# Layer 0's adaLN weights by column groups, and five tiles' latents summed with features outermost

## The chip, the cores and the metric

The kernel runs on one core of a Trainium2 chip, as one launch. A core has a matrix engine (TensorE, PE in the profile, with weight loads listed apart as PEld), three engines for elementwise work (VectorE or DVE, ScalarE or ACT, GpSimd or POOL), and SyncE (SP), whose queue issues most of the transfers between the chip's memory and the core's on-chip memory. The metric is the device time of the launch in microseconds; lower is better.

## The reference, cut to what matters

A two-layer diffusion backbone over 1024 latent tokens and 256 context tokens, 1024 features wide. Each layer modulates its input with a shift and a scale that come out of a conditioning vector; the context has a vector of its own.

```python
def adaln(cvec, w, b):
    m = jax.nn.silu(cvec) @ w + b                    # w: 1024 x 3072, b: 3072
    return jnp.split(m, 3, axis=-1)                  # shift, scale, gate

shift, scale, gate = adaln(c, ada_w[i], ada_b[i])
shift_c, scale_c, gate_c = adaln(c_ctx, ada_w[i], ada_b[i])
h = x * (1.0 + scale[:, None, :]) + shift[:, None, :]
h_c = ctx * (1.0 + scale_c) + shift_c
...
# layer 0, multi-head latent attention
q_lat, kv_lat, k_pe, gate = jnp.split(t @ w_in, splits, axis=-1)     # 256, 128, 32, 1024 columns
q = (rms_norm(q_lat, g_qa) @ w_qb).reshape(bsz, n, A_HEADS, A_NOPE + A_ROPE)
kv = (rms_norm(kv_lat, g_kva) @ w_kvb).reshape(bsz, n, A_HEADS, A_NOPE + A_V)
```

For this document the first steps of layer 0 matter: the shift and the scale of both vectors, h for all 1280 tokens, and the first 416 columns of `h @ w_in`, called the latents. The gates (the other 1024 columns), the attention, and layer 1 (differential attention) follow and are the same in both kernels.

## The kernel before

All matrix work of layer 0 up to here is in f32 accuracy: each operand is split into a high part, rounded for TensorE's fast f32 mode, and a low part, the rest. One product is three matmuls (`mm3`, lines 216 to 219: high x high, high x low, low x high).

The 1280 tokens are 10 tiles of 128: tiles 0 to 7 the latents of the image, 8 and 9 the context. Features are 8 blocks of 128, k = 0 to 7. h is held transposed, features on the partitions: `hH` and `hL`. Its parts come in three chunks of tokens (`CHUNKS`): 0 to 511 (tiles 0 to 3), 512 to 1023 (tiles 4 to 7) and the 256 context tokens. One part (`h_part`, line 286) is a load, ScalarE's modulation into `hH` (line 292), the same sum once more by VectorE (293), and a subtraction into `hL` (295) on VectorE, or GpSimd for every third k.

The order before:

- The adaLN weights come by rows: for each k a tile of 128 x 1024 for the scale, then one for the shift (line 254, `adaw`, a ring of 6). One row block holds all columns, so no scale and no shift is complete before the last block is there. The scale is summed by TensorE (line 260), 8 matmuls of 128 x 128 each block, as a column over the partitions; the bias enters by matmuls over one row (line 243). The shift is summed by VectorE (line 264), two products of 1024 columns for each k, one for each vector, into `hacc`; line 273 turns it into columns with 8 matmuls for each vector. `cols0` holds the finished columns.
- The input weights (`in_weight`, line 245, 128 x 416 each) come between, split into `wAH` (line 208) and `wAL` (line 209).
- Then h of the context, the first half of tile 8's latents (`lat_mm`, line 279: for a tile, for each k, one `mm3`), the image's shift, h of the first chunk, and the second half.
- A loop over the tiles 8, 9, 0, ..., 7 then sums a tile's 24 latent matmuls, normalises it (lines 405 to 412: squares on ScalarE, a power on GpSimd, products on VectorE) and, three tiles later, turns it (`lat_post`, transposes in lines 378 and 379 into a bank of kind c, of which there are two; copy in 380, subtraction in 381, copy in 384, and a small store in 385). In the same loop the second chunk of h is made and the first gate weights are loaded (`gate_w`, line 353). The last three turns alternate with the first three gate tiles (`gate_tile`, 24 matmuls of 256 columns).
- Then come the remaining gate tiles, each beside one step of side work: the up weights (line 428 on, their column sums in line 450) and layer 1's adaLN (`ada_dve`).

Order: in this part TensorE's instructions stay in the order of the program (`manual_schedule`, `MAN = 'P'`). Those of the other engines and of SP's queue are placed by the framework's scheduler, by priority (program order, raised inside `high_priority`) and its own estimate of when operands are ready. On the chip each of them runs in that fixed order. A tile from a ring (`bufs`) is written again once its readers are done.

## Time and profile before

| What | Value |
|---|---|
| Median of three runs | 1677.8 us (1677.79 to 1680.78) |
| Profiled execution, its own time | 1678.12 us |
| Its span in the profile | 1676.3 us |
| TensorE busy | 1610.6 us, 96% of the span |
| VectorE, ScalarE, GpSimd busy | 1264.0, 1144.2, 908.8 us |
| Mean granted clock of TensorE | 0.993 |
| Transfers over the span | 171.63 MB, mean 102 GB/s |
| adaLN weight loads of layer 0 | 16 of 512 KB |

How to read it: times in the views are microseconds from the start of the span. L260 is line 260 of the kernel before. A row such as `PE ps_c L260 <- DMA adaw<-in_ada_w: 4.8, 3, 2.7` says that TensorE's instruction of that line waited for that transfer, 4.8 us in all, three times, at most 2.7 us. A row of a group ends with its busy time, the mean of one in ns, the idle time of the engine before it and what ended it. A row of stretches gives the stretch, its length, the busy time and the count of instructions for each engine, the granted clock, the busy share of the 16 DMA engines, and GB/s. A matmul in f32 shows as two records. Neighbouring records of TensorE overlap, since each includes the time until its result is out.

### The profile page before, as it was taken

The numbers are of one execution on the slowest core, as the hardware profiler recorded it, in microseconds if no ns is written. First come the engines' busy times: TensorE is split into PE (matmuls) and PEld (weight loads), VectorE is DVE, ScalarE is ACT, GpSimd is POOL, SyncE is SP. The second block draws the span as 40 slices with busy tenths as digits, with TensorE's granted clock in tenths as the row PEclk, the third lists the DMA queues.
The fourth block names the chain that finished last, engine by engine and source line by source line (L and its number), as shares of the span: only waits on it lengthen the run. The fifth ranks groups of instructions, "written<-read, shape, count | busy, mean of one in ns | idle before, by whom it ended". The sixth has DMA issues, their size and how long they took to land.

```text
span 1676.3 us, 36592 instructions
## 1 busy us (share of the span) xinstructions
PE 1610.6 (96%) x14308; PEld 1205.2 (72%) x14308; DVE 1264.0 (75%) x2005; ACT 1144.2 (68%) x2228; POOL 908.8 (54%) x772
## 2 busy tenths in 40 slices
PE   7999999999999999989999999999999999996998
PEld 6999966666666666667776686767686868674776
DVE  7657856776676766855763989999889889888685
ACT  2652148878888788936554888878788787877352
POOL 1523027877777777855644526262635454555565
PEclk9999999999999999999999999999999999998999
DMA  9347620111111121346533244444443333253542
GB/s 319 91 132 232 206 81 21 42 33 42 39 36 42 39 52 45 104 167 204 177 113 79 72 101 102 102 102 105 98 95 86 96 84 92 59 156 89 146 135 76
DMA packets 183932, 171.63 MB, mean 102 GB/s; under 512 B 82024, under 2 KB 159432, under 8 KB 183759
## 3 DMA queue, kind: packets, MB, share of 16 engines
q1 hardware_dynamic: 175886, 161.96, 35.1%
q10 hardware_dynamic: 7872, 7.34, 1.3%
q8 instruction: 112, 1.84, 0.5%
q14 instruction: 62, 0.50, 0.1%
HBM read 98.65 MB, written 27.07 MB: 75 GB/s over the span
## 4 chain that ended last, share of the span: by engine, by line
PE 65%; DVE 19%; ACT 9%; issue 3%; DMA 2%; POOL 2%; POOLq 0%; DVEq 0%; SPq 0%; ACTq 0%
PE ps_s L217 5%; PE ps_s L219 5%; PE ps_s L218 5%; PE ps_a L969 4%; PE ps_a L970 4%; PE ps_a L971 4%; PE ps_a L217 3%; PE ps_a L219 3%; PE ps_a L218 3%; ACT p L1874 3%; PE ps_a L920 3%; DVE mx L1867 3%; DVE p L1887 3%; PE ps_d L994 2%; PE ps_d L987 2%
## 5 line engine op out<-in xcount | busy, mean ns | idle before, releaser
L979 POOL TENSOR_TENSOR pl<-p,ph 128x1024 f16<-128x1024 f32 (+1 forms) x176 | 370.2, 2117 | 102.7 <-ACT ph L977 68.6
L975 ACT ACTIVATE p<-ps_a,esc 128x1024 f32<-128x1024 f32 (+1 forms) x176 | 188.7, 1072 | 58.9 <-PE ps_a L971 52.4
L924 DVE TENSOR_REDUCE mx<-ps_a 128x1 f32<-128x1024 f32 x128 | 156.2, 1222 | 72.1 <-PE ps_a L920 71.5
L1874 ACT ACTIVATE p<-ps_p,mx 128x512 f32<-128x512 f32 x256 | 175.5, 689 | 31.4 <-DVE mx L1869 30.6
L977 ACT CAST ph<-p 128x1024 f16<-128x1024 f32 (+1 forms) x176 | 177.0, 1006 | 7.0 <-PE ps_d L988 1.8
L1867 DVE TENSOR_REDUCE mx<-ps_p 128x1 f32<-128x512 f32 x256 | 164.2, 680 | 1.9 <-PE ps_p L1846 1.9
L969 PE MATMUL ps_a<-qH,KH 100*128 100x512 f16 x320 | 122.0, 381 | 3.1 <-DVE mx L924 2.3
L970 PE MATMUL ps_a<-qH,KL 96*128 96x512 f16 x320 | 121.5, 380 | 0.0
L971 PE MATMUL ps_a<-qL,KH 96*128 96x512 f16 x320 | 120.7, 377 | 0.0
L1795 DVE SCALAR_TENSOR_TENSOR pl<-ps_t,lcf,ph 128x512 f16<-128x512 f32 (+1 forms) x128 | 78.2, 611 | 42.5 <-ACT ph L1793 41.9
L1887 DVE SCALAR_TENSOR_TENSOR p<-p,sm,p 128x1280 f32<-128x1280 f32 x64 | 106.1, 1658 | 1.7
L1845 PE MATMUL ps_p<-KS,QS 128*128 128x512 f16 x256 | 98.1, 383 | 9.5 <-ACT p L1874 9.5
L987 PE MATMUL ps_d<-Vh,ph 128*128 128x65 f16 x1344 | 103.7, 194 | 2.0 <-ACT ph L977 1.7
L988 PE MATMUL ps_d<-Vl,ph 128*128 128x64 f16 x1344 | 103.2, 194 | 0.0
L1793 ACT ACTIVATE ph<-ps_t,lcf 128x512 f16<-128x512 f32 (+1 forms) x128 | 74.8, 584 | 39.3 <-PE ps_t L1788 38.1
L1846 PE MATMUL ps_p<-KS,Q 128*128 128x512 f16 x256 | 98.2, 383 | 0.0
L987 PEld LDWEIGHTS <-ph 128*128 128x128 f16 x1344 | 89.0, 98 | 11.2 <-issue 4.8
L988 PEld LDWEIGHTS <-ph 128*128 128x128 f16 x1344 | 87.3, 98 | 3.8
L191 POOL TENSOR_SCALAR ss<-ss 128x1 f32<-128x1 f32 x64 | 20.4, 318 | 119.1 <-ACT ps_t L1817 117.4
L920 PE MATMUL ps_a<-KH,qH 96*128 96x512 f16 x256 | 76.1, 379 | 0.0
L936 DVE TENSOR_REDUCE mx<-ps_a 128x4 f32<-128x1024 f32 (+1 forms) x48 | 50.3, 1048 | 33.9 <-PE ps_a L931 33.9
L1810 PE MATMUL ps_t<-vh,ph 128*128 128x128 f16 x384 | 68.4, 221 | 6.4 <-DVE pl L1795 6.3
(503 smaller groups left out, 5573.3 us busy)
## 6 DMA issues: line engine op xcount, KB each, us to landing
ws<-in_dw SPq DMA_DIRECT2D x28, 512.0 KB, 3.9
adw<-in_ada_w SPq DMA_DIRECT2D x24, 512.0 KB, 4.5
adaw<-in_ada_w SPq DMA_DIRECT2D x16, 512.0 KB, 6.8
g<-sg_d SPq DMA_DIRECT2D x16, 512.0 KB, 3.5
sg_d<-gg ACTq DMA_DIRECT2D x40, 128.0 KB, 2.9
o_d<-op SPq DMA_DIRECT2D x7, 640.0 KB, 3.8
xt<-in_xT SPq DMA_DIRECT2D x16, 256.0 KB, 3.7
wgs<-in_w_in SPq DMA_DIRECT2D x32, 128.0 KB, 2.9
```

Source lines behind the costliest of these rows:

```text
L924: add("m.max", "D", 1.223, lambda t=t, ps=ps: dve.tensor_reduce(mx.tile[:, t, 0:1], ps.tile, axis=AX.X, op=ALU.max), r=[ps], w=[(mx, t)] i ...
L969: pe.matmul(s_, KH[i][:nr, ks], QH.tile[:nr, :], start=True, stop=False)
L970: pe.matmul(s_, KL[i][:DQ, ks], QH.tile[:DQ, :], start=False, stop=False)
L971: pe.matmul(s_, KH[i][:DQ, ks], QLo.tile[:DQ, :], start=False, stop=True)
L975: add("s.exp", "A", 1.114 if x else 0.682, lambda st=st, p32=p32: act.activation(p32.tile[:, :2 * n], st.tile[:, :2 * n], AF.Exp, scale=esc0),
L977: add("s.hi", "A", 1.046 if x else 0.618, lambda p32=p32, ph=ph: act.copy(ph.tile[:, :2 * n], p32.tile[:, :2 * n]), r=[p32], new=[ph], hol ...
L979: add("s.lo", "G", 2.14 if x else 1.17, lambda p32=p32, ph=ph, pl=pl: pool.tensor_tensor(pl.tile[:, :2 * n], p32.tile[:, :2 * n], ph.tile[ ...
L987: pe.matmul(v_()[:, t, :], w, Vh[:, k, h, :], start=(k == kcs[0] and t == 0), stop=False, skip_group_check=True)
L988: pe.matmul(v_()[:, t, :V0], w, Vl[:, k, h, :], start=False, stop=False, skip_group_check=True)
L1867: add(f"max{m}", "D", 0.68, lambda i=i, b_=b_: dve.tensor_reduce(mx.tile[:, 2 + 2 * m + i:3 + 2 * m + i], b_.tile, axis=AX.X, op=ALU.max, ...
L1874: add(f"exp{m}", "A", 0.78 if n == 512 else 0.57, lambda i=i, c0=c0, n=n, b=b, lo=lo: act.activation(p[m].tile[:, c0:c0 + n], b.tile[:, lo ...
L1887: add("join", "D", 1.65, lambda: dve.scalar_tensor_tensor(p[0].tile, p[1].tile, sm.tile[:, 4:5], p[0].tile, op0=ALU.mult, op1=ALU.add), r= ...
```

## The change

The features form five groups, given as first block and number of blocks: (0, 1), (1, 1), (2, 2), (4, 2), (6, 2). For a group only the columns of its features are loaded, over all 1024 rows (`ada_load`): tiles of 128 x 1024 as before, but a row of a transfer is 128 or 256 numbers, 512 or 1024 bytes, instead of 4 KB. The ring has 7 tiles.

- A group's scale is summed on TensorE, 8 matmuls for each block. For the first three groups (features 0 to 3) the shift is too. For the last two, VectorE sums the shift with high priority, 16 products of 256 columns for each group, and TensorE turns it with matmuls of one column.
- The bias comes as 16 rows of 128, is turned once, and is added when the sums leave PSUM. The matmuls of line 243, the four warm-up matmuls of line 301 and `shift_cols` go.
- Behind each group follow, for each of its features, the input weight, h of the context and h of the first chunk. For odd features GpSimd makes `wAL` and subtracts for `hL`; ScalarE makes the second modulation of the first chunk. The second chunk of h follows for all features.
- Five tiles (8, 9, 0, 1, 2) have a bank of their own from the start, and a feature's latent matmuls are issued for all five once the next group's adaLN sums have been issued; a group of two adds its own first feature's. Features 6 and 7 come last.
- Tiles 3 to 7 are summed after that, one by one, as before. Between them come turns of earlier tiles; four turns stand in a row after tile 7, then one gate tile, then the last two turns. Each turn takes two steps of the gate weights instead of one.
- The side work begins at the fourth gate tile, as before, by a test on the count of gate tiles.

The diff:

```diff
@@ -228,60 +228,79 @@
 
     hs_ctx = ExitStack()
     hs = hs_ctx.enter_context(spool("hstage", side="right"))
-    rowb = hs.tile([P, D], F32, tag="adaw", bufs=6, name="rowb")[0:1, :]
-    acc = [hs.tile([P, D], F32, name=f"hacc{s}") for s in range(2)]
-    sp.dma_start(rowb, ada_b[0:1, D:2 * D])
-    for s in range(2):
-        pool.memset(acc[s], 0.0)
+    GROUPS = (0, 1), (1, 1), (2, 2), (4, 2), (6, 2)
+    EARLY = 8, 9, 0, 1, 2
+    bt = cpool.tile([16, P], F32, tag="bt", name="bt")
+    sp.dma_start(bt, ada_b[0:1, :2 * D].rearrange("o (k p) -> (o k) p", p=P))
     man = ExitStack()
     man.enter_context(tc.manual_schedule(engines={ENG[c] for c in MAN}))
-    cbs = [bank("c").rearrange("p (j n) -> p j n", j=4) for _ in range(2)]
     scb = hs.tile([P, KT, P], F32, name="scb")
     pool.tensor_copy(scb.rearrange("p k (n s) -> p k n s", s=2),
                      sc.rearrange("p (k o s) -> p k o s", o=1, s=2).to_broadcast([P, KT, 64, 2]))
-    for j in range(KT):
-        pe.matmul(cbs[j // 4][:, j % 4, :], rowb[:, j * P:(j + 1) * P], ones[0:1, :], start=(j % 4 == 0), stop=False,
-                  skip_group_check=True)
+    bcol = cpool.tile([P, 16], F32, tag="bcol", name="bcol")
+    bk = bank("c")
+    pe.transpose(bk[:, :16], bt, idn[:16, :16])
+    dve.tensor_copy(bcol[:, 0:8], bk[:, 0:8])
+    dve.tensor_scalar_add(bcol[:, 8:16], bk[:, 8:16], 1.0)
+
+    def ada_load(k0, nk, g):
+        n, per = nk * P, KT // nk
+        ws = []
+        for q in range(nk):
+            w = hs.tile([P, D], F32, tag="adaw", bufs=7, name=nm("adaw")).rearrange("p (c n) -> p c n", n=n)
+            c0 = g * D + k0 * P
+            sp.dma_start(w, ada_w[0, q * per * P:(q + 1) * per * P, c0:c0 + n].rearrange("(c p) n -> p c n", p=P))
+            ws += [w[:, c, :] for c in range(per)]
+        return ws
 
     def in_weight(k):
         ws = hs.tile([P, 512], F32, tag="xt", bufs=14, name=nm("ws"))
         sp.dma_start(ws[:, :NA], w_in[k * P:(k + 1) * P, :NA])
-        split(wAH[:, k, :], wAL[:, k, :], ws[:, :NA], e_lo=pool if k > 5 else None)
-
-    for k in range(KT):
-        for g in (1, 0):
-            w = hs.tile([P, D], F32, tag="adaw", bufs=6, name=nm("adaw"))
-            sp.dma_start(w, ada_w[0, k * P:(k + 1) * P, g * D:(g + 1) * D])
-            if k == 0 and g == 0:
-                for s in range(2):
-                    sp.dma_start(acc[s][0:1, :], ada_b[0:1, :D])
-            if g:
-                for j in range(KT):
-                    pe.matmul(cbs[j // 4][:, j % 4, :], w[:, j * P:(j + 1) * P], scb[:, k, :], start=False,
-                              stop=(k == KT - 1), skip_group_check=True)
-            else:
-                for s in (1, 0):
-                    dve.scalar_tensor_tensor(acc[s], w, sc[:, 2 * k + s:2 * k + s + 1], acc[s], op0=ALU.mult, op1=ALU.add)
-        if k > 1:
-            in_weight(k - 2)
-    for i in range(2):
-        dve.tensor_scalar_add(cols0[:, 8 + 4 * i:12 + 4 * i, :], cbs[i][:, :, 0:2], 1.0)
-
-    def shift_cols(s):
-        cb = bank("d")
-        for j in range(KT):
-            pe.matmul(cb[:, 32 * j:32 * j + P], acc[s][:, j * P:(j + 1) * P], ones, start=True, stop=True)
+        split(wAH[:, k, :], wAL[:, k, :], ws[:, :NA], e_lo=pool if k % 2 else None)
+
+    def bias2(j0, nk):
+        return bcol[:, j0:j0 + nk].rearrange("p (a o) -> p a o", o=1).to_broadcast([P, nk, 2])
+
+    def ada_cols(k0, nk, whole):
+
+        n = nk * P
+        w1_ = ada_load(k0, nk, 1)
+        w0_ = ada_load(k0, nk, 0)
+
+        def summed(ws):
+            cb = bank("c").rearrange("p (j n) -> p j n", j=4)
+            for c in range(KT):
+                for j in range(nk):
+                    pe.matmul(cb[:, j, :], ws[c][:, j * P:(j + 1) * P], scb[:, c, :], start=(c == 0 and j == 0),
+                              stop=(c == KT - 1), skip_group_check=True)
+            return cb[:, :nk, 0:2]
+
+        def keep(j0, src):
+            with tc.high_priority():
+                dve.tensor_tensor(cols0[:, j0:j0 + nk, :], src, bias2(j0, nk), op=ALU.add)
+
+        scale = summed(w1_)
+        if whole:
+            keep(8 + k0, scale)
+            keep(k0, summed(w0_))
+            return
+        acc = [hs.tile([P, 256], F32, tag="hacc", bufs=4, name=nm("hacc"))[:, :n] for _ in range(2)]
         with tc.high_priority():
-            dve.tensor_copy(cols0[:, 0:8, s], cb[:, :256].rearrange("p (j n) -> p j n", j=KT)[:, :, 0])
+            for s in (1, 0):
+                dve.tensor_scalar_mul(acc[s], w0_[0], sc[:, s:s + 1])
+                for c in range(1, KT):
+                    dve.scalar_tensor_tensor(acc[s], w0_[c], sc[:, 2 * c + s:2 * c + s + 1], acc[s], op0=ALU.mult, op1=ALU.add)
+        keep(8 + k0, scale)
+        cb = bank("c")
+        for s in (1, 0):
+            for j in range(nk):
+                pe.matmul(cb[:, 2 * j + s:2 * j + s + 1], acc[s][:, j * P:(j + 1) * P], ones[:, 0:1], start=True, stop=True)
+        keep(k0, cb[:, :2 * nk].rearrange("p (j s) -> p j s", s=2))
 
     def lat_mm(ps, t, ks):
         ts = slice(t * P, (t + 1) * P)
         for k in ks:
             mm3(ps[:, :NA], hH[:, k, ts], hL[:, k, ts], wAH[:, k, :], wAL[:, k, :], k == 0, k == KT - 1)
-
-    shift_cols(1)
-    for k in (6, 7):
-        in_weight(k)
 
     def h_part(pool_, bufs, c0, n, k):
 
@@ -290,20 +309,32 @@
         sp.dma_start(xt[:, :n], xT[k * P:(k + 1) * P, c0:c0 + n] if s == 0 else ctxT[k * P:(k + 1) * P, :])
         hi = hH[:, k, c0:c0 + n]
         act.activation(hi, xt[:, :n], AF.Identity, bias=cols0[:, k, s:s + 1], scale=cols0[:, 8 + k, s:s + 1])
-        dve.tensor_scalar(xt[:, :n], xt[:, :n], cols0[:, 8 + k, s:s + 1], cols0[:, k, s:s + 1],
-                          op0=ALU.mult, op1=ALU.add)
-        (pool if k % 3 == 2 else dve).tensor_tensor(hL[:, k, c0:c0 + n], xt[:, :n], fv(hi), op=ALU.subtract)
-
+        if c0 == 0 and k % 2:
+            act.activation(xt[:, :n], xt[:, :n], AF.Identity, bias=cols0[:, k, s:s + 1], scale=cols0[:, 8 + k, s:s + 1])
+        else:
+            dve.tensor_scalar(xt[:, :n], xt[:, :n], cols0[:, 8 + k, s:s + 1], cols0[:, k, s:s + 1],
+                              op0=ALU.mult, op1=ALU.add)
+        (pool if k % 2 else dve).tensor_tensor(hL[:, k, c0:c0 + n], xt[:, :n], fv(hi), op=ALU.subtract)
+
+    early = {t: bank(b_) for t, b_ in zip(EARLY, "abdab")}
+
+    def lat_of(*ks):
+        for t in EARLY:
+            lat_mm(early[t], t, ks)
+
+    for i, (k0, nk) in enumerate(GROUPS):
+        ada_cols(k0, nk, i < 3)
+        for k in range(k0, k0 + nk):
+            in_weight(k)
+            for c in (CHUNKS[2], CHUNKS[0]):
+                h_part(hs, 14, *c, k)
+        if i:
+            lat_of(k0 - 1)
+        if 0 < i < len(GROUPS) - 1 and nk == 2:
+            lat_of(k0)
     for k in range(KT):
-        h_part(hs, 14, *CHUNKS[2], k)
-    ps8 = bank("a")
-    for _ in range(4):
-        pe.matmul(ps8[:, :NA], idr, wAH[:, 0, :], start=True, stop=True)
-    lat_mm(ps8, 8, range(4))
-    shift_cols(0)
-    for k in range(KT):
-        h_part(hs, 14, *CHUNKS[0], k)
-    lat_mm(ps8, 8, range(4, KT))
+        h_part(hs, 14, *CHUNKS[1], k)
+    lat_of(6, 7)
     hs_ctx.close()
     upw = rp.enter_context(spool("upw", side="right"))
     wqH = upw.tile([P, 2, 1536], F32R, name="wqH")
@@ -384,21 +415,9 @@
             act.copy(kpt, tp[:ROPE, 384:512])
             sp.dma_start(kp_d[:, ts], kpt)
 
-        hk = iter(range(KT))
-        todo = []
-        for t in (8, 9, 0, 1, 2, 3, 4, 5, 6, 7, None, None, None):
-            if len(todo) == 3 or t is None:
-                lat_post(*todo.pop(0))
-                next(gw, None)
-            if t is None:
-                for _ in gw:
-                    pass
-                gate_tile(0, *wg)
-                continue
-            ps = ps8
-            if t != 8:
-                ps = bank("a" if t % 2 == 0 else "b")
-                lat_mm(ps, t, range(KT))
+        pend = []
+
+        def norm(t, ps):
             with tc.high_priority():
                 junk = pa.tile([P, QL], F32, tag="junk", bufs=1, name=nm("junk"))
                 ss = pa.tile([P, 2], F32, tag="ss", bufs=3, name=nm("ss"))
@@ -410,10 +429,35 @@
                 dve.tensor_scalar_mul(ln[:, :QL], ps[:, :QL], rs[:, 0:1])
                 dve.tensor_scalar_mul(ln[:, QL:QL + KVL], ps[:, QL:QL + KVL], rs[:, 1:2])
                 act.copy(ln[:, QL + KVL:], ps[:, QL + KVL:NA])
-            todo.append((t, ln))
-            for k in (next(hk, None), next(hk, None)):
-                if k is not None:
-                    h_part(pa, 3, *CHUNKS[1], k)
+            pend.append((t, ln))
+
+        def post():
+            lat_post(*pend.pop(0))
+            next(gw, None)
+            next(gw, None)
+
+        def late(t, b_):
+            ps = bank(b_)
+            lat_mm(ps, t, range(KT))
+            return ps
+
+        for t in EARLY[:4]:
+            norm(t, early[t])
+        ps = late(3, "d")
+        post()
+        norm(2, early[2])
+        for t, b_ in ((4, "a"), (5, "b"), (6, "d"), (7, "a")):
+            ps2 = late(t, b_)
+            post()
+            norm(t - 1, ps)
+            ps = ps2
+        norm(7, ps)
+        while pend:
+            if len(pend) == 2:
+                for _ in gw:
+                    pass
+                gate_tile(0, *wg)
+            post()
     wa_ctx.close()
 
     def up_weights(pa):
@@ -614,7 +658,8 @@
                 gate_tile(q, wH, wL)
                 if gcount[q] > 1:
                     next(gw, None)
-                next(side, None)
+                if sum(gcount) > 3:
+                    next(side, None)
         for _ in chain(gw, side):
             pass
     p0.close()
```

## The prediction

> **What bounds the kernel now.** I read the page first, then the busy time by stretch over the first 220 us (all that the diff touches lies there), then TensorE's waits, then the transfers. On the page, in 40 slices, TensorE is busy nearly throughout; the weak slices are the first one and a few later.
>
> ```profile
> PE   7999999999999999989999999999999999996998
> ```
>
> The stretches (us; per engine busy us and count, then granted clock, DMA share, GB/s):
>
> ```profile
> 0.00:7.86 7.86, 3.70 (x16) 3.48 (x16) 0.60 (x2) 1.80 (x3) 3.30 (x10) 1.00 0.63 205
> 7.86:24.15 16.29, 14.19 (x97) 13.61 (x96) 13.53 (x13) 1.62 (x3) 0.00 (x0) 1.00 1.00 377
> 24.15:39.99 15.84, 11.62 (x66) 9.97 (x67) 13.78 (x22) 6.72 (x13) 4.08 (x3) 0.89 0.95 325
> 39.99:63.25 23.26, 23.26 (x134) 22.66 (x134) 19.67 (x37) 15.21 (x40) 12.98 (x16) 1.00 0.39 117
> ...
> 85.19:110.00 24.81, 24.35 (x196) 24.04 (x194) 10.10 (x19) 11.91 (x32) 6.65 (x11) 1.00 0.60 176
> 110.00:130.00 20.00, 17.52 (x130) 16.22 (x131) 12.88 (x26) 10.81 (x24) 5.12 (x10) 1.00 0.34 94
> 130.00:220.00 90.00, 90.00 (x732) 86.62 (x731) 67.03 (x72) 16.03 (x40) 17.47 (x14) 1.00 0.69 204
> ```
>
> Two regimes: until 40 us the transfers are full (share 0.95 to 1.00) and TensorE lacks 10.5 us of 40; from 40 us TensorE is full, apart from 2.9 us between 85 and 130. So whatever TensorE finishes earlier at 63 us arrives at 220 us undiminished unless those 2.9 us change. Its waits, to 45 us and from 40 to 130 us:
>
> ```profile
> PE ps_c L260 <- DMA adaw<-in_ada_w: 4.8, 3, 2.7
> PE ps_c L243 <- POOL ones L185: 4.2, 1, 4.2
> PE ps_a L217 <- ACT hH L292: 0.5, 1, 0.5
> ```
> ```profile
> PE ps_c L450 <- ACT wsq L439: 1.6, 1, 1.6
> PE ps_c L450 <- DVE u L326: 1.3, 1, 1.3
> ```
>
> The chain of waits gives the mark I measure against:
>
> ```profile
> 53.13 0.41 PE ps_c L378 x3
> ...
> 63.25 0.33 PE ps_c L378 x3
> ...
> 83.14 0.33 PE ps_c L378 x3
> ```
>
> L378 is the transpose of one tile's latents. From 53.13 to 83.14 there are six rounds, 5.00 us each: 24 latent matmuls (0.19 us each, 4.57 us) and one transpose group (0.4 us). At 63.25 the five tiles 8, 9, 0, 1, 2 are summed and two transposes are done. The changed kernel reaches its five sums with none done, so its equal point is 63.25 - 0.8 = **62.4 us**.
>
> **The change part by part: TensorE's work up to that point.** Going from features innermost to outermost keeps the 120 latent matmuls: 120 x 0.19 = 22.8 us. Removed are the 16 records of L243 (3.8 us), four warm-up matmuls (1.0 us) and 32 records of the shift transposes (4.0 us). Added are 32 shift matmuls for the features 0 to 3, like the 64 scale ones: 96 altogether, two records each. Their price, and what the cold start costs (matmuls of line L260 by stretch; TensorE, weight loads, clock, share, GB/s):
>
> ```profile
> 18.94 2.05 PE L260 MATMUL ps_c<-scb,adaw 128*128 128x128 f32 x16 [1.00 <-DMA adaw<-in_ada_w]
> ```
> ```profile
> 7.86:9.86 2.00, 1.99 (x9) 2.00 (x10) 1.00 1.03 416
> 9.86:11.86 2.00, 2.00 (x11) 2.00 (x10) 1.00 1.02 401
> 11.86:13.86 2.00, 2.00 (x13) 2.00 (x12) 1.00 0.81 189
> 13.86:15.86 2.00, 2.00 (x20) 2.00 (x19) 1.00 1.00 403
> ...
> 26.85:28.85 2.00, 2.00 (x10) 2.00 (x11) 0.57 1.02 402
> ```
>
> Sixteen records take 2.05 us, the last one's 0.27 us of drain included: (2.05 - 0.27) / 15 = 0.118 us each, so 192 records cost 22.7 us. The first 6 us of this work went at half that pace (33 records where 50 would fit): 33 x 0.118 = 3.9 us, 2.1 us more than needed. I charge the 2.1 us once; after the 2.7 us wait before 26.85 the granted clock fell to 0.57 again, and with latent matmuls between the groups there should be no such gap.
> [...]
>
> The last two groups' shift is summed on VectorE and turned by 8 matmuls (16 records) of one column; before does such a thing at L518, 16 records in 1.68 us (chain of waits). First group's weights: the first shift product waited for the second 0.5 MB tile and began at 7.49.
>
> ```profile
> 159.29 1.68 PE ps_c L518 x16
> ```
> ```profile
> 7.49 2.48 DVE L264 SCALAR_TENSOR_TENSOR hacc<-adaw,sc,hacc 128x1024 f32<-128x1024 f32 x2 [3.64 <-DMA adaw<-in_ada_w]
> ```
>
> The first tile is there one tile time before that: 0.52 MB at 400 GB/s, 1.3 us, so 6.2 us; with rows of 512 B, 0.5 us later, 6.7 (below). Sum: 6.7 + 22.7 + 2.1 + 1.7 + 22.8 + 0.1 (bias transpose) = **56.1 us** if TensorE never waits again. I add 1.4 us for waits where a group's columns hand over (three times the 0.5 us of L217 above): 57.5, a gain of **4.9 us**.
>
> **Do the transfers keep up?** Rows become 512 B (four tiles) and 1 KB (twelve) instead of 4 KB. Nearest rows: a lone load with 1 KB rows (L1576, seen from 881 to 884 us), a store with 512 B rows (L1009, 326 to 331) and a transposing one with 256 B packets (926 to 934); per view busy tenths, then GB/s:
>
> ```profile
> DMA  2398669899999999997643310000000000000000
> GB/s 82 123 246 205 246 218 287 287 369 382 341 369 396 423 355 369 369 314 259 232 164 123 109 41 27 27 0 0 0 0 0 0 0 0 0 0 0 0 0 0
> ```
> ```profile
> DMA  0296202502007899999999999999992000000000
> GB/s 0 82 229 156 58 0 74 164 25 66 0 16 221 270 291 299 291 291 299 299 287 291 295 295 291 291 299 283 287 271 78 0 0 0 0 0 0 0 0 0
> ```
> ```profile
> GB/s 0 0 0 0 0 0 0 0 0 0 0 0 0 0 0 0 0 0 0 0 0 0 0 0 0 113 228 212 209 211 202 132 4 0 0 0 0 0 82 0
> ```
>
> At full share: 365 GB/s at 1 KB, 291 at 512 B, bounds 211 (256 B) and 400 (4 KB rows above). A tile of 0.52 MB takes 1.44 or 1.8 us. Behind each feature come 0.61 MB (416 + 256 + 512 columns of 128 rows in f32) at some 355 GB/s, 1.71 us. With the flow starting at 3.4 us the last adaLN tile lands at 3.4 + 4 x 1.8 + 12 x 1.44 + 6 x 1.71 + 1 = 39 us. By the sum above TensorE ends groups 0 and 1 at 12.6 and 16.4 us, feature 0's latents at 19.2, group 2 at 26.8, its latents at 32.5, the scale of 4 and 5 at 36.2, latents at 42.8, the scale of 6 and 7 at 46.5. The last tile must be there 3.4 us of VectorE (half a group's products, below) before that: 43.1. Slack 4.0 us. In the ring of 7 that tile waits for the first half of the scale of 4 and 5, read by 34.4, so it holds nothing up.
> SP issues as many loads as before, in another order. The eight of the third chunk now stand ahead of the small constants, which nobody needs yet; their 2.1 MB follow the last 1.2 MB and land near 49 us, for tile 4 at 62.
>
> **VectorE, ScalarE, GpSimd.** Sixteen products of 1024 columns (19.8 us) become 32 of 256:
>
> ```profile
> L264 DVE SCALAR_TENSOR_TENSOR hacc<-adaw,sc,hacc 128x1024 f32<-128x1024 f32 x16 | 19.8, 1282 | 7.5 <-DMA adaw<-in_ada_w 7.4
> L381 DVE TENSOR_TENSOR latL<-ps_c,latH 128x384 fp32r<-128x384 f32 x10 | 5.5, 551 | 5.0 <-ACT latH L380 5.0
> L380 ACT CAST latH<-ps_c 128x384 fp32r<-128x384 f32 x10 | 4.7, 470 | 0.4 <-ACT gg L368 0.4
> L295 POOL TENSOR_TENSOR hL<-xt,hH 128x512 fp32r<-128x512 f32 x4 | 6.0, 1501 | 6.6 <-DVE xt L293 6.6
> L384 ACT COPY kpt<-ps_c 32x128 f32<-32x128 f32 x10 | 2.5, 252 | 2.0 <-DVE latL L381 2.0
> ```
>
> At 0.43 us each (between a quarter of 1282 and the 551 ns of 384 columns) 32 cost 13.8 us, less than before. Moving the odd features' arithmetic to ScalarE and GpSimd, and the third chunk of h ahead of the tiles, adds nothing to these engines that 50 us of TensorE would not hide; if that cover is gone, the price is the stall in the rivals.
>
> **Behind the five sums.** The order there changes: after tile 7's matmuls four transposes follow in a row instead of one. Each holds one of two banks for a copy, a subtraction and a copy: 0.47 + 0.55 + 0.25 us and 0.4 of TensorE, about 1.7 us; the third and fourth wait, some 1.7 us lost (bounds 0 and 2.6, two banks in turn without any overlap). On the other side the last transpose stands one gate tile earlier ahead of the loads of the up weights (SP's queue, behind the stores of line 385): 24 matmuls 0.12 us apart in the chain of waits, 2.9 us.
>
> ```profile
> 112.11 0.12 PE ps_d L218
> ```
>
> So the first L450 wait (1.6 us) should go, the second (1.3) perhaps: 0 to 2.9, I take 1.6. Together -0.1. The `sum(gcount) > 3` test keeps the number of side steps and their place in TensorE's order: nothing.
>
> So 4.9 - 0.1 = 4.8 us less: the profiled 1678.1 becomes 1673.3, and against the median of the runs, 0.3 lower, **1673.0 us**. Without the 1.4 us and with both L450 waits gone and no loss at the transposes the gain is 6.3 + 2.9 = 9.2: 1668.6.
>
> **Rivals.** *A, hand-over waits*: the sums of VectorE, or the odd features on GpSimd (1.5 us for a 512-column subtraction), come late for each of the five groups. Another 0.8 us for each group takes 4.0 of the 4.8: 1677.0. For it: VectorE runs in a fixed order. Against: 50 us of cover.
> *B, transfers bound*: a load at small rows in a full queue may be slower than a lone one. At 211 GB/s for 512 B (2.5 us a tile) and 250 for 1 KB (2.1 us; halfway to 291) the last tile comes 4 x 0.7 + 12 x 0.66 = 10.7 us later, 6.7 after the slack; gain 4.8 - 6.7: 1679.7. It decides from 4.0 us of delay on. Against: 1 KB at 365.
> [...]
> *C, the other side, slower*: the products for features 4 and 5 carry high priority. If they stand on VectorE ahead of h of feature 2 and wait for their weights, feature 2's latents wait too. Their second tile needs the middle of group 2 free and lands at about 30; eight products (3.4 us), twice, end at 35.5; h two instructions later, 36.7. TensorE wanted it at 29.7: 7.0 us. The same in the last group, whose tile is then requested late: about 2.9. Together 9.9, so 4.8 - 9.9: 1682.9. It decides from 4.8 us of stall on.
> *D, given back later*: four transposes cost 2.6, the L450 waits stay and SP holds the up weights: 4.9 - 2.6 - 1: 1676.5.
>
> **How the numbers follow.** My forecast 0.52 (1668.5 to 1675.5), A 0.17, B 0.08, C 0.14, D 0.09. The range 1668.0 to 1681.5 leaves out most of C and a little of each end. About 0.2% (3.4 us) is what can be told from no change: faster means under 1674.4. Of the forecast nine tenths lie there, of A and D a fifth: 0.52. Slower (over 1681.2): C and a piece of B, 0.17. The rest, 0.31, is no change.
>
> **What would show it.** Right: latent matmuls from about 16 us on, TensorE without a gap over 1 us between 7 and 57 us, five sums done by 57.5, L378 in a row of four near 82, L450 waits below 1.5 us. Wrong: TensorE waiting for `adaw` after 15 us (B), for hH or hL at L217 and L219 before 40 us while VectorE waits for `adaw` (C), or the lead at 63 us not found again at 130 us (D).

## The result and the profile after

The changed kernel takes 1689.7 us (median of 6 runs, 1687.73 to 1696.87) against 1678.11 for the kernel before beside it: ratio 1.0075 with a 95% interval of 1.0055 to 1.0095. It is slower by 11.6 us. 1673.0 was forecast, and the range ended at 1681.5.

The profiled execution of the changed kernel took 1687.73 us with a span of 1685.9 us, 9.6 us more than the span before. The lines have moved: the scale and shift matmuls are L274, VectorE's products L290 and L292, the one-column matmuls L297, the finished columns L280, h L311 to L317, the turns L409 to L416, the normalising L424 to L431, the up weights' column sums L494, and layer 1's one-column matmuls L562.

The same stretches as before (per engine busy us and count, granted clock, DMA share, GB/s):

```profile
7.86:24.15 16.29, 16.20 (x129) 16.03 (x128) 4.21 (x12) 5.04 (x8) 3.11 (x3) 1.00 1.11 343
24.15:39.99 15.84, 13.34 (x92) 13.06 (x91) 11.15 (x27) 6.28 (x11) 5.47 (x4) 1.00 1.09 353
39.99:63.25 23.26, 21.25 (x113) 20.72 (x112) 22.00 (x42) 13.97 (x28) 9.88 (x8) 0.85 0.46 148
...
85.19:110.00 24.81, 21.36 (x152) 20.84 (x151) 7.47 (x15) 10.84 (x34) 6.60 (x10) 0.86 0.48 138
110.00:130.00 20.00, 17.96 (x135) 17.41 (x135) 14.46 (x26) 9.85 (x19) 0.38 (x2) 0.91 0.33 101
```

To 24 us the change does what was hoped: TensorE is busy 16.2 of 16.3 us in the second stretch, where it was 14.2. In the third it is ahead still, 13.3 us busy against 11.6, though 2.5 us idle. The fourth turns round: 2.0 us idle where it had none, VectorE now busy 22.0 of 23.3 us, and the granted clock at 0.85. In three stretches in which the clock was 1.00 it has fallen.

TensorE's waits to 140 us (us in total, times, longest), then the clock in stretches of 2 us:

```profile
PE ps_c L297 <- DVE hacc L292: 4.5, 3, 2.0
...
PE ps_c L409 <- ACT kpt L415: 3.5, 1, 3.5
PE ps_c L274 <- DMA adaw<-in_ada_w: 2.6, 1, 2.6
PE ps_c L494 <- DVE vm L498: 2.0, 1, 2.0
PE ps_c L409 <- DVE ln L429: 0.7, 1, 0.7
```
```profile
50.00:52.00 2.00, 2.00 (x10) 1.97 (x11) 1.19 (x4) 0.69 (x2) 0.00 (x0) 0.58 0.41 82
52.00:54.00 2.00, 2.00 (x7) 1.90 (x7) 2.00 (x5) 2.00 (x4) 0.00 (x0) 0.50 0.67 185
...
92.00:94.00 2.00, 1.71 (x9) 1.58 (x9) 0.46 (x2) 1.28 (x5) 1.54 (x3) 0.50 0.55 132
...
96.00:98.00 2.00, 2.00 (x11) 2.00 (x11) 0.00 (x0) 0.78 (x3) 1.24 (x2) 0.50 0.31 79
```

Three places stand out. The only wait for weights is the first one, 2.6 us. The one-column matmuls waited 4.5 us for VectorE's products, the third turn of the row 3.5 us, and the column sums 2.0 us. After the wait that ended at 49.74 and after the row of turns the clock was 0.50: 7 records of latents in 2 us, where e4 below has 12 at full clock (54 to 56 us).

Two marks split the loss. The first turn began at 67.72, after its own wait of 0.67 and one tile of latents (4.57 us), so the five sums ended at 67.72 - 0.67 - 4.57 = 62.5 us. The equal point before is 62.4: the whole forecast gain was gone by then. Layer 1's one-column matmuls, in the chain of waits, stand at 165.90 where they stood at 159.29:

```profile
67.72 0.59 PE ps_c L409 x3
...
165.90 1.68 PE ps_c L562 x16
```

So 6.6 us were lost at 160 us: 0.1 at the five sums and 6.5 between there and 160 us. The remaining 3.0 of the span's 9.6 us came after 1500 us, in code that the diff doesn't touch.

Why the products are late is seen in VectorE's own order (start, busy, idle time before in brackets):

```profile
29.82 1.09 DVE L290 TENSOR_SCALAR hacc<-adaw,sc 128x256 f32<-128x256 f32 x2 [1.17 <-DMA adaw<-in_ada_w]
30.84 4.43 DVE L292 SCALAR_TENSOR_TENSOR hacc<-adaw,sc,hacc 128x256 f32<-128x256 f32 x11
...
38.46 0.16 DVE L280 TENSOR_TENSOR cols<-ps_c,bcol 128x4 f32<-128x4 f32 x1 [0.70 <-PE ps_c L297]
39.29 0.41 DVE L315 TENSOR_SCALAR xt<-xt,cols 128x256 f32<-128x256 f32 x1 [0.67 <-ACT hH L311]
...
41.46 2.13 DVE L290 TENSOR_SCALAR hacc<-adaw,sc 128x256 f32<-128x256 f32 x2
43.52 6.47 DVE L292 SCALAR_TENSOR_TENSOR hacc<-adaw,sc,hacc 128x256 f32<-128x256 f32 x14
...
51.11 0.16 DVE L280 TENSOR_TENSOR cols<-ps_c,bcol 128x4 f32<-128x4 f32 x1 [0.55 <-PE ps_c L297]
```

From 29.8 to 51.1 VectorE is one chain nearly without a gap: products for the features 4 and 5 (8 us), their columns, h of feature 4, products for 6 and 7 (8.5 us), their columns. The last columns are there at 51.3, and ScalarE, which needs them for h, had stood idle 5.45 us. It then had 8 us of modulations in a row, those of the second chunk (tokens 512 to 1023, called the third in the prediction) among them:

```profile
51.31 3.21 ACT L311 ACTIVATE hH<-xt,cols 128x256 fp32r<-128x256 f32 x5 [5.45 <-DVE cols L280]
...
55.13 4.33 ACT L311 ACTIVATE hH<-xt,cols 128x512 fp32r<-128x512 f32 x6
```

Part of the chain's length may not be the products' own. Taken one by one, 27 of the 32 products last 0.34 to 0.47 us. The other five last longer (0.83 us at 29.82, 1.17 at 35.30, 0.83 and 1.38 at 41.46 and 42.22, 1.33 at 43.52), and each of these runs beside a subtraction that the change gave to GpSimd. GpSimd's rows in the last group:

```profile
41.03 2.42 POOL L317 TENSOR_TENSOR hL<-xt,hH 128x256 fp32r<-128x256 f32 x2 [4.84 <-DVE xt L315]
43.48 1.09 POOL L209 TENSOR_TENSOR wAL<-ws,wAH 128x416 fp32r<-128x416 f32 x1
```

Against the pace of the others the five took some 3.6 us more, 2.4 of them in the last group, where TensorE waited 2.0 us. That GpSimd's work lengthens them is read from these rows; no run here moved the subtractions away, so it is not shown.

The row of turns, all engines:

```profile
88.24 0.49 PE L409 MATMUL ps_c<-idr,ln 128*128 128x128 f32 x3
...
88.93 0.73 POOL L209 TENSOR_TENSOR wgL<-wgs,wgH 128x256 fp32r<-128x256 f32 x1 [3.88 <-ACT wgH L208]
89.01 0.86 ACT L411 CAST latH<-ps_c 128x384 fp32r<-128x384 f32 x2
...
90.02 0.69 POOL L192 TENSOR_TENSOR rs<-rs,neghalf 128x2 f32<-128x2 f32 x1
...
90.74 0.48 DVE L429 TENSOR_SCALAR ln<-ps_a,rs 128x256 f32<-128x256 f32 x1 [1.50 <-POOL rs L192]
...
91.40 1.01 DVE L412 TENSOR_TENSOR latL<-ps_c,latH 128x384 fp32r<-128x384 f32 x2
...
92.29 0.90 PE L409 MATMUL ps_c<-idr,ln 128*128 128x128 f32 x3 [3.45 <-ACT kpt L415]
```

The first two turns hold both banks of kind c. Their subtractions (L412) stand on VectorE behind the normalising of tile 7, which waits for GpSimd's power (L192), which stands behind a gate weight (L209). The subtractions could have begun at 89.9, when ScalarE's copies were done; they began at 91.40.

### The profile page after: what moved, and what is told of

Its sections match the earlier page's. It is cut to its first block, busy times and chain, and to the rows that moved or that the text cites. A ratio compares the mean times of both kernels' runs of the same rounds, so it can differ in the third digit from the quotient of the medians.

```text
span 1685.9 us, 36684 instructions
## 1 busy us (share of the span) xinstructions
PE 1616.8 (96%) x14337; PEld 1212.4 (72%) x14337; DVE 1255.6 (74%) x2017; ACT 1148.7 (68%) x2232; POOL 917.3 (54%) x778
## 4 chain that ended last, share of the span: by engine, by line
PE 61%; DVE 20%; ACT 11%; issue 3%; DMA 3%; POOL 3%; SPq 0%; POOLq 0%; DVEq 0%; ACTq 0%
ACT p L1919 4%; PE ps_a L1014 4%; PE ps_a L1015 4%; PE ps_a L1016 4%; PE ps_s L217 4%; PE ps_s L219 4%; PE ps_s L218 4%; PE ps_a L217 3%; PE ps_a L218 3%; PE ps_a L219 3%; DVE mx L1912 3%; PE ps_a L965 3%; DVE p L1932 3%; PE ps_d L1039 2%; PE ps_d L1032 2%
## 5 line engine op out<-in xcount | busy, mean ns | idle before, releaser
L1919 ACT ACTIVATE p<-ps_p,mx 128x512 f32<-128x512 f32 x256 | 175.7, 690 | 30.4 <-DVE mx L1914 29.8
```

The source lines that it names most:

```text
L1919: add(f"exp{m}", "A", 0.78 if n == 512 else 0.57, lambda i=i, c0=c0, n=n, b=b, lo=lo: act.activation(p[m].tile[:, c0:c0 + n], b.tile[:, lo ...
```

## The experiments

Unless a text says otherwise, an edit is to the changed kernel. "Mark" is the start of layer 1's one-column matmuls (159.29 before). The columns give the mark's and the run's difference to the kernel before; a mark comes from one profiled execution, a run from the median of all.

| Kernel | Edit | Mark | Run | Ratio, 95% interval |
|---|---|---|---|---|
| changed | none | +6.6 | +11.6 | 1.0075 (1.0055 to 1.0095) |
| e1_cover | latents ahead of the one-column matmuls | +5.3 | +9.2 | 1.0054 (1.0040 to 1.0068) |
| e2_turns | turns spread | +3.5 | +7.0 | 1.0036 (1.0023 to 1.0049) |
| e3_both | e1 and e2 | +1.6 | +4.9 | 1.0028 (1.0019 to 1.0037) |
| e4_fill | unread matmuls in the two waits | +6.3 | +9.8 | 1.0051 (1.0039 to 1.0063) |
| e5_last | VectorE sums groups 3 and 4, with cover | +7.2 | +9.7 | 1.0056 (1.0041 to 1.0071) |
| e6_last_turns | e5 and e2 | +2.1 | +2.8 | 1.0020 (1.0011 to 1.0029) |
| e7_shift | before, delayed by 6.3 us | +6.7 | +7.5 | 1.0045 (1.0032 to 1.0058) |
| e8_nosum | 28 of 32 products out | +3.2 | +4.4 | 1.0028 (1.0017 to 1.0038) |
| e9_allpe_turns | all shift on TensorE, and e2 | +6.2 | +8.1 | 1.0041 (1.0028 to 1.0053) |
| e10_nosum_turns | e8 and e2 | -3.1 | -0.2 | 1.0001 (0.9990 to 1.0011) |
| e11_row | before, with the row of turns | +3.7 | +8.5 | 1.0043 (1.0028 to 1.0058) |
| e12_shift8 | before, delayed by 1.5 us | +3.3 | +1.7 | 1.0012 (1.0001 to 1.0022) |
| e13_shift16 | before, delayed by 3.1 us | +1.6 | +3.6 | 1.0020 (1.0011 to 1.0030) |
| e14_shift50 | before, delayed by 9.5 us | +9.6 | +15.9 | 1.0095 (1.0074 to 1.0117) |

A mark also holds the half clock that fell ahead of it, and where that falls is not the edit's alone: in e2, whose edit lies behind the five sums, the clock was 0.50 from 40 to 42 us and 1.00 from 50 to 54, the other way round than in the changed kernel. A difference of 1.7 to 3.4 us between two marks is therefore not shown to come from an edit unless a wait in the trace accounts for it.

**Covering the hand-over (e1_cover).**

```diff
         keep(8 + k0, scale)
+        mid()
         cb = bank("c")
...
-        if i:
+        if 0 < i < 3:
             lat_of(k0 - 1)
```

`mid()` issues the latents of feature k0 - 1.

> The changed kernel, with one change of TensorE's order: in the last two groups the latents of the feature before (3, 5) are issued between the scale matmuls and the one-column matmuls that wait for VectorE's sums. Theory W (short waits of TensorE, each followed by some 6 us at half clock): the waits of 2.5 us near 37 us and of 2.0 us near 48 us go, and with the second the half clock from 51 to 57 us (3.2 us); the five sums end near 57 instead of 62.4 us, and the kernel gains 5 to 7 us on the changed one (about 1683). Rival Q (the sums are late because VectorE or the transfers are the limit): the matmuls only wait at another place, and the gain is under 1.5 us.

The wait for the products is gone (0.2 us left), but waits for h stand in its place. TensorE's waits:

```profile
PE ps_a L217 <- ACT hH L312: 2.6, 2, 1.7
...
PE ps_a L219 <- DVE hL L318: 1.7, 2, 1.4
```

Work put into the gap only moved the gap, since the latents behind it waited for the same late columns. The first turn came at 69.08 without a wait of its own, so the five sums ended at 69.08 - 4.57 = 64.5 us, 2.0 later than in the changed kernel: theory W is refuted. The 1.3 us of the mark were gained behind them, where less low clock fell: 1.7 us lost between 90 and 100 us instead of 3.4, and none behind the column sums. The row of turns still waited 3.4 us and the column sums 2.4.

**Spreading the turns (e2_turns, e3_both).**

```diff
             ps2 = late(t, b_)
             post()
+            if t < 7:
+                post()
```

> The changed kernel, with the turns spread: two follow each of the tiles 4, 5 and 6, so that one stands behind tile 7, then a gate tile, then two. Theory W: the wait of 3.45 us near 89 us and the half clock behind it (2.9 us) go, so 5 to 6.3 us less than the changed kernel (about 1683.5). Rival Q (ScalarE, VectorE and GpSimd need that time for the turns and the norms anyway): the wait moves, and the gain is under 2 us.

> Both orders together. Theory W: the two gains add, 10 to 13 us, so 1677 to 1679, level with the kernel before; the third wait, at the column sums near 123 us (2.0 us and 1.5 us of half clock), may stay. Rival Q: within 3 us of the changed kernel.

e2 takes 3.1 us off the mark and 4.6 off the run (5 to 6.3 expected): the wait of 3.5 in the row goes, and the half clock behind it. New waits eat part of it, 2.9 us in three for the copies and 2.0 for a normalising. With both edits the mark is 5.0 us earlier than in the changed kernel, about what the two give apart (1.3 and 3.1) and a little more, and still 1.6 us later than before. The run stays 4.9 us above, where theory W had it level.

**Is it the wait or the half clock? (e4_fill).** Twelve unread matmuls ahead of the last group's one-column matmuls and twenty between the second and third turn keep TensorE busy through the two waits.

```diff
+        if k0 == 6:
+            for _ in range(12):
+                pe.matmul(cb[:, 64:64 + NA], idr, wAH[:, 0, :], start=True, stop=True)
...
+            if len(pend) == 4:
+                dm = bank("d")
+                for _ in range(20):
+                    pe.matmul(dm[:, :NA], idr, wAH[:, 0, :], start=True, stop=True)
```

> The changed kernel in its own order, with matmuls whose result nobody reads in the two places where TensorE waits: 12 ahead of the one-column matmuls of the last group, 20 between the second and the third turn of the row (0.19 us each, 2.3 and 3.8 us at full clock, so they end about with the waits). They take no wait away and add work. Theory W, in which more than 6 us of the loss is the half clock that follows a wait: granted clock 1.0 throughout from 15 to 110 us, and 4.5 to 6 us less than the changed kernel. Rival Q (the waits alone cost the time): no gain, 0 to 1 us more.

The mark moved by 0.3 us. From 44 us on the clock stayed at 1.00, but not before: after the waits near 37 us, which are not filled, it was 0.50. Stretches of 2 us, ScalarE's modulations, and the first turn:

```profile
40.00:42.00 2.00, 2.00 (x7) 1.93 (x7) 1.72 (x5) 2.00 (x4) 0.02 (x1) 0.50 1.09 374
...
54.00:56.00 2.00, 2.00 (x12) 2.00 (x12) 2.00 (x4) 2.00 (x5) 1.53 (x1) 1.00 0.06 19
56.00:58.00 2.00, 1.45 (x7) 0.74 (x5) 2.00 (x5) 2.00 (x4) 0.42 (x1) 1.00 0.00 0
58.00:60.00 2.00, 1.26 (x7) 1.25 (x8) 1.97 (x6) 2.00 (x4) 1.64 (x2) 1.00 0.00 0
```
```profile
53.55 3.21 ACT L314 ACTIVATE hH<-xt,cols 128x256 fp32r<-128x256 f32 x5 [6.40 <-DVE cols L280]
...
69.56 0.49 PE L412 MATMUL ps_c<-idr,ln 128*128 128x128 f32 x3
```

The last columns came 2.2 us later than in the changed kernel (53.55 against 51.31). Of this 1.0 us was there already at the first one-column matmuls (37.57 against 36.62); the rest is the filler's. From the last columns to the first turn it then took 69.56 - 53.55 = 16.0 us at full clock. In the changed kernel, with the half clock, it took 67.72 - 0.67 - 51.31 = 15.7 us. The order of h's instructions differs a little between the two, so the 0.3 us are not to be read. But in this stage full clock saved nothing: from 54 to 60 us VectorE and ScalarE are busy throughout, and up to 62 us TensorE waits 2.5 us for hL instead. The engines that make h set the pace. Behind the row of turns the half clock did cost: from the third turn to the fifth it took 6.4 us in the changed kernel (92.29 to 98.71) and 3.7 us here (94.07 to 97.78). The run lies 1.8 us nearer to the kernel before than the changed kernel's, between what the two theories said. That the half clock alone was the loss is refuted.

**Other places for VectorE's sums (e5_last, e6_last_turns).** VectorE sums the shift of the features 2 to 5, TensorE that of 0, 1, 6 and 7, with the cover of e1; e6 adds the spread turns.

```diff
-        ada_cols(k0, nk, i < 3)
+        ada_cols(k0, nk, i in (0, 1, 4), lambda: lat_of(k0 - 1))
...
-        if i:
+        if i in (1, 4):
             lat_of(k0 - 1)
```

> The changed kernel with VectorE's shift sums for features 2 to 5 in place of 4 to 7: the last group's shift (6, 7) is now summed by TensorE, group (2, 2) by VectorE, and in both of VectorE's groups the latents of the feature before stand ahead of the one-column matmuls. The same amount of work for each engine. Theory V (the chain of VectorE, 16 products, h, 16 products, h, from 30 to 51 us, sets the end of the five sums; covering its waits alone moved nothing): the five sums end at 57 to 59 us instead of 62.4, no half clock between 40 and 64 us, and 4 to 6 us less than the changed kernel. Rival H (h of the last two features on ScalarE, VectorE and GpSimd sets it, wherever the sums are): 60 us or later, and less than 2 us gained.

> The same with the turns spread as before. Theory V: the gains of both add up, 8 to 11 us less than the changed kernel, 1679 to 1682, so level with the kernel before or up to 3 us behind. Rival H: as with spread turns alone, 1685.

In e5 the waits went to the front, 1.9 us for the products and 1.8 for hH, with low clock from 28 to 36 us, and the first turn came at 69.03 (68.18 in e6; 67.72 in the changed kernel). With that turn waiting for nothing, the five sums of e5 ended at 69.03 - 4.57 = 64.5 us, as rival H has it, and not at 57 to 59. Moving the products does not help the five sums. e6 is, at 1.0020, the nearest to the kernel before of all versions of the change that compute the whole reference, though its interval overlaps that of e3, and it does not beat the kernel before.

**Taking the products away (e8_nosum).** Only the first of eight products stays for each group and vector.

```diff
-                for c in range(1, KT):
+                for c in range(1, 1):
```

> The changed kernel without 28 of the 32 products of VectorE's shift sums: for features 4 to 7 only the first block of rows is taken, seven eighths of the sum are left out, and their shift is wrong. All transfers, matmuls and orders stay. Theory V: five sums done at 57 to 58 us as in the forecast's sum, no wait at the one-column matmuls and full clock from 15 us to the row of turns; 4 to 6 us less than the changed kernel. Rival B (transfers) or H: still 60 us or later.

TensorE's waits, and the first turn:

```profile
PE ps_c L409 <- ACT kpt L415: 3.5, 1, 3.5
PE ps_c L409 <- DVE ln L429: 2.8, 1, 2.8
PE ps_c L494 <- DVE vm L498: 2.6, 1, 2.6
```
```profile
63.90 0.90 PE L409 MATMUL ps_c<-idr,ln 128*128 128x128 f32 x3 [2.77 <-DVE ln L429]
```

The five sums ended at 63.90 - 2.77 - 4.57 = 56.6 us, between the forecast's 56.1 without waits and 57.5 with them; one wait of 1.3 us, for a subtraction of GpSimd, is in it. So the sum over TensorE was right, and with the products the five sums end 5.9 us later, at 62.5. Further on it is lost again: the row of turns, the normalising and the column sums wait 8.9 us, and the mark is 3.2 us later than before. The normalising of tile 8 waits because GpSimd's power for it begins at 62.62, right behind the last of GpSimd's subtractions for the second chunk (60.62 to 62.26).

**Both removed (e10_nosum_turns).** e8 and e2 together.

> The changed kernel with 28 of the 32 products left out (the shift of the features 4 to 7 is not the reference's), and with two turns after the tiles 4, 5 and 6. e8 did the first alone (mark 162.52), e2 the second (162.80), against 165.90. Theory T (the two costs are apart and add): 165.90 - 3.38 - 3.10 = 159.4, level with before; run within 3 us of before. Rival F (with both gone the forecast's gain of 4.9 us stands): mark at 154 to 156, run 3 to 5 us below before. Rival R (a third thing behind both, the column sums of the up weights, holds them): a wait of 3 us or more at these sums and the mark at 161 or later.

The chain of waits:

```profile
62.87 0.59 PE ps_c L409 x3
...
156.15 1.68 PE ps_c L564 x16
```

The mark is 3.1 us ahead of before, 9.8 ahead of the changed kernel: more than the two edits gave apart (3.4 and 3.1), and short of the forecast's gain of 4.9. The normalising still holds the first turn 2.8 us. So without these two places the whole loss of 6.6 us against the kernel before is gone at 160 us. How the 3.3 us beyond the sum of the two edits arise was not taken apart; the changed kernel has low clock at 50 to 57, 92 to 98 and 124 to 130 us, e10 only at 62 to 68. The run is nevertheless only level with before.

**The row of turns by itself (e11_row).** The kernel before, with its front as it was.

```diff
-            if len(todo) == 3 or t is None:
-                lat_post(*todo.pop(0))
+            if len(todo) == 4:
+                lat_post(*todo.pop(0))
...
+        for _ in range(3):
+            lat_post(*todo.pop(0))
```

> The kernel before, with its front untouched, and each turn one place later, so that four turns stand in a row behind tile 7 (then one gate tile, one turn, two gate tiles). Theory T (the row of turns costs by itself, because its copies and subtractions stand in fixed orders behind the normalising of tile 7): a wait of 2 us or more at the third turn, mark (159.29) later by 3 to 6.5 us, run 3 to 9 us slower. Rival N (the row costs only behind the changed front, whose engines are late): waits of the row under 1.5 us in all, mark within 1.5 us, run within 2.5 us. The forecast's own price was 1.7 us.

TensorE's third turn, and the clock:

```profile
91.39 0.55 PE L378 MATMUL ps_c<-idr,ln 128*128 128x128 f32 x3 [3.45 <-ACT kpt L384]
```
```profile
92.00:94.00 2.00, 2.00 (x11) 1.94 (x11) 1.02 (x2) 1.56 (x5) 0.83 (x2) 0.50 0.59 142
```

The same 3.45 us as in the changed kernel, without its front: the row has this price by itself, as theory T said. With the half clock it moves the mark by 3.7 us.

**All of the shift on TensorE (e9_allpe_turns).**

```diff
-        ada_cols(k0, nk, i < 3)
+        ada_cols(k0, nk, True)
...
             post()
+            if t < 7:
+                post()
```

> The changed kernel with the shift of all five groups summed on TensorE (32 more matmuls of 128 x 128, no products on VectorE, no matmuls of one column), and with two turns instead of one after the tiles 4, 5 and 6. TensorE's own work grows by 64 records x 0.118 - 1.7 = 5.9 us against the same kernel without products (e8, five sums at about 56.6 us). Theory T (TensorE full, VectorE's products were only ever a way to save it these 5.9 us): no wait for hacc, five sums at 62 to 63 us, first turn near 67.5, no half clock between 46 and 100 us, the mark (layer 1's one-column matmuls, 159.29 before, 165.90 in the changed kernel) at 160 to 161.5, run 1 to 4 us above before. Rival R (the waits come back at h's engines, as in e1 and e4): waits of 2 us or more for hH or hL, five sums after 63.5, mark at 162.5 or later, run 4 to 7 us above before.

No product is left, yet TensorE waited 2.4 us for VectorE's hL and 1.3 for GpSimd's at 56 and 58 us. The clock was low in the stretches from 56 to 66 us, and the first turn began at 70.48 without a wait, so the five sums ended at 65.9, as rival R has it. The run was 8.1 us slower than before, above both ranges. TensorE's longer sums delay the last columns just as the products did (ScalarE got them at 52.21), and h then has to be made with nothing else to do.

**Is the late part the change's? (e7_shift, e12 to e14).** The kernel before with 33, 8, 16 or 50 unread matmuls ahead of tile 9.

```diff
+        dm = bank("b")
+        for _ in range(33):
+            pe.matmul(dm[:, :NA], idr, wAH[:, 0, :], start=True, stop=True)
```

> The kernel before, with 33 matmuls ahead of tile 9's latents whose result nobody reads: 6.3 us of TensorE that nothing else hides, and no other change. In the profile of the changed kernel TensorE is 6.6 us behind at the first one-column matmuls near 160 us, but 9.6 us at the end, and the clock is low for 3 us more in the last stages. Theory S (what comes late there is the same for any kernel that arrives some us later: the low clock depends on when a wait falls): 8 to 10 us more than the kernel before. Rival N (the late part belongs to the change): 6 to 6.5 us more.

> The kernel before with 8 unread matmuls (0.19 us each, 1.5 us) ahead of tile 9, nothing else. Theory L (what runs after 220 us costs another time according to when it begins, since the half clock after its waits comes in stretches of fixed length): the run is later by something else than the delay, between 0 and 5 us, and in the profile the lost clock after 700 us (9.3 us in the profile before) accounts for the difference. Rival N (a delay is handed on one to one): run 0.5 to 2.5 us later, lost clock after 700 us as before.

> The same with 16 unread matmuls, 3.1 us. Theory L: run later by something else than the delay, between 1 and 7 us, the excess found in the lost clock after 700 us or in another half clock between 60 and 220 us. Rival N: run 2 to 4 us later.

> The same with 50 unread matmuls, 9.5 us. Theory L: run later by 9 to 14 us, not in step with 6.3 us giving 7.5. Rival N: run 8.5 to 10.5 us later. Were every delay dearer by the same 1 to 3 us, whatever its size, it would not be the phase but that any shift leaves a placement that suits the kernel before (theory M): then all three, and the 6.3 us of e7, lie 1 to 3 us over their delay.

Delays of 1.5, 3.1, 6.3 and 9.5 us made the run 1.7, 3.6, 7.5 and 15.9 us later. The small ones pass on nearly one to one, as rival N said, the largest does not, and no theory had its size; theory M, the same 1 to 3 us over each delay, is out (0.2, 0.5, 1.2 and 6.4 us over). In the profiles all four lose another 1.2 to 3.6 us between 1500 us and 1640 us against the profile before, as the changed kernel does (2.9), and as e10 does (4.1). Stretches of the kernel before, the changed kernel and e10 there:

```profile
1530.00:1540.00 10.00, 5.53 (x40) 3.96 (x39) 7.56 (x12) 8.01 (x14) 3.49 (x4) 0.66 0.92 242
1540.00:1550.00 10.00, 6.56 (x33) 4.82 (x34) 9.19 (x13) 5.99 (x18) 9.91 (x5) 1.00 0.34 84
```
```profile
1530.00:1540.00 10.00, 5.72 (x42) 4.49 (x42) 8.83 (x11) 6.97 (x18) 7.38 (x6) 0.83 0.23 50
1540.00:1550.00 10.00, 6.41 (x41) 4.93 (x41) 8.76 (x11) 7.66 (x16) 6.50 (x3) 0.60 0.68 195
```
```profile
1530.00:1540.00 10.00, 5.86 (x43) 4.49 (x43) 7.84 (x12) 8.52 (x17) 5.72 (x3) 0.75 0.74 212
1540.00:1550.00 10.00, 8.20 (x29) 5.59 (x28) 9.89 (x12) 5.10 (x16) 8.07 (x7) 0.66 0.48 131
```

The code there is the same, and TensorE has waits in all three; low clock falls on more of it in the last two (from 1530 to 1550 us 3.4 us lost before, 1.7 + 4.0 in the changed kernel, 2.5 + 3.4 in e10). A plain delay brings more of it too, and e6, a version of the change, loses nothing behind its mark (mark 2.1 us later, span 2.3), so these 3 us are not shown to be the change's. What decides how much of that stage falls under the half clock stays open, and with it why 9.5 us became 15.9 and why e10's lead of 3.1 us is not found in its run.

## Why the prediction was wrong

- **The sum over TensorE to the five sums (56.1 us): right.** First weights at 6.5 against 6.7, and 56.6 in all once the products were out of the way (e8), 1.3 us of waiting for hL included. Only the 2.1 us charged for the slow start were too much: the first 32 records took 5.17 us from 6.50 on and 3.73 from 44.00 on, so 1.4.
- **The transfers (slack 4.0 us): right.** TensorE never waited for weights after the first ones, and VectorE 1.2 us once (29.82); the queue ran at 343 and 353 GB/s from 8 to 40 us. Rival B is out.
- **"Adds nothing to these engines that 50 us of TensorE would not hide": the step that failed first.** The products took 16.1 us (12.9 for the 28 of L292, 3.2 for the 4 of L290) against 13.8 forecast; five of them, beside GpSimd's subtractions, account for more than the difference. But the size was the lesser part. They cannot be spread under 50 us: they begin when their weights are there (29.8), and the second block stands behind the first block's columns and h. That chain ends at 51.1, where the forecast's sum has TensorE through the last group's scale at 46.5. I never added VectorE's instructions up in their order. The 1.4 us for hand-overs became 4.5 us of waits, and the late columns then kept ScalarE at h until 59 us and VectorE until 64. The odd features' subtractions on GpSimd were not free either: once the products were out, TensorE waited 1.3 us for one of them, and 2.8 us for the normalising behind them (e8).
- **That "there should be no such gap": wrong, as a consequence.** A gap of 2.0 us at 47.7 to 49.7 was followed by half clock to 57. By e4 that half clock had no price of its own up to the first turn (15.7 us with it, 16.0 without), since h was no earlier.
- **Rival C** had the right engine and the right sign, and the wrong order: h of feature 4 came ahead of the last products, not behind them. Its 1682.9 lies nearest to the result of all cases. **Rival A** named the mechanism of the front, sums of VectorE that come late, but spread it over five groups at 0.8 us each; it took place in the two groups that have such sums, at 2.5 and 2.0 us.
- **The "about 1.7 us" for the four turns (bounds 0 and 2.6): too small and bounds too narrow.** It measured 3.45 us and a stretch of half clock, by itself too (e11). I costed a turn as its own three operations, and left out that its subtraction stands on VectorE behind the normalising of the tile just summed, which stands behind GpSimd.
- **The L450 waits (1.6 us less):** 2.9 us before, 2.0 after, so 0.9 less, and a half clock of 1.7 us behind it that wasn't there before.
- **Rival D** named the place of the second loss, at 2.6 + 1 us where 6.5 were lost.

The 16.7 us between 1673.0 and 1689.7 split so: 5.0 up to the five sums, 6.4 from there to 160 us (6.5 lost, 0.1 forecast), 3.0 after 1500 us in the profile, 2.0 between the profiled run and the median of its kernel, and 0.3 by which the kernel before stood higher beside it.

## What to carry to other kernels

A sum over the busiest engine gives only the lower bound of a stage (the five sums ended at 56.6 us in e8 and at 62.5 with the products); where another engine has to hand it something, list that engine's instructions in their own order, from the moment its first operand lands, and see when the last one is done. A step that is repeated back to back costs not its own operations but all that stands in front of them in each engine's own order (3.45 us at the third turn, in the changed kernel and in e11), so look for what was issued just before. Work moved into a gap did not shorten a chain that runs on other engines (the five sums at 64.5 us in e1 and 65.9 in e9; 16.0 us from the last columns to the first turn in e4, 15.7 in the changed kernel).

## What the runs showed of the hardware

Waits of 2.0 us were followed by the half clock (2.01 us up to 49.74 and 2.04 up to 124.89 in the changed kernel, 2.03 up to 116.34 in e7), but the length of the wait does not decide alone. In the same place, the column sums of the up weights, a wait of 2.03 us in e7 was followed by it, and one of 2.21 us in e14 was not:

```profile
116.34 0.51 PE L453 MATMUL ps_c<-wsq,onr 128*128 128x512 f32 x1 [2.03 <-ACT wsq L442]
```
```profile
118.00:120.00 2.00, 2.00 (x11) 2.00 (x11) 1.99 (x5) 0.00 (x0) 0.00 (x0) 0.50 0.34 111
```
```profile
120.34 0.51 PE L453 MATMUL ps_c<-wsq,onr 128*128 128x512 f32 x1 [2.21 <-ACT wsq L442]
```
```profile
122.00:124.00 2.00, 2.00 (x19) 2.00 (x18) 1.87 (x5) 0.51 (x2) 0.00 (x0) 1.00 0.35 115
```

Even the same waits in the same place do not always bring it. The first one-column matmuls waited 1.88 and 0.62 us both in the changed kernel (from 36.62) and in e4 (from 37.57). The clock stayed at 1.00 in the first and was 0.50 from 40 to 42 us in the second.

Added up over stretches of 2 us in the nine profiles read from end to end (before, changed, e5 to e8, e12 to e14), the lost clock of one such event was 1.7 us or a multiple: 1.7 in the kernel before (26 to 32 us), 3.4 and 5.1 in the changed kernel (50 to 58 and 1540 to 1554), 6.8 in e5 (1546 to 1562); only what the end of a span cuts off did not fit (0.8 from 1672 us on in the kernel before). At a clock of 0.50, 1.7 us lost are some 3.4 us of half clock. What sets that length no run here shows.

The 256-column product on VectorE had no fixed price. Undisturbed it took 0.40 us from one start to the next (8 in a row from 30.84, 13 from 44.77), and 0.83 to 1.38 us in the five cases named above, each of which ran beside a subtraction of GpSimd. Three others (34.01 to 35.27) that overlap GpSimd's subtraction at 34.17 kept their 0.40 us, and that subtraction took 2.01 us where the like one at 43.48 took 1.09. Which engine holds up the other, and why, was not tested.
